# One 64-column product per level and chunk in the chunked HGRN2 recurrence, in place of merged 192-column products

## The chip, the cores and the metric

One core of a Trainium2 chip runs the whole kernel. The metric is the device time of one execution in microseconds (us). The kernel before took 1265.52 us, the median of three runs (1264.85 to 1266.1).

## What is computed

The reference is one decoder layer on 1024 tokens of width 1024, in float32: RMSNorm, one input projection (3584 columns), two head groups side by side, one output projection with residual, then RMSNorm, a SwiGLU feed-forward of hidden width 2816, residual and a last RMSNorm. Group A is dilated softmax attention with rotary positions (8 heads of 64). Group B, which the change touches, is HGRN2 (4 heads, state 128):

```python
f = lb + (1.0 - lb) * jax.nn.sigmoid(f_logit)
key = 1.0 - f
qf = jax.nn.silu(q)
# S_t = diag(f_t) S_{t-1} + (1 - f_t) i_t^T,  o_t = S_t^T q_t, computed chunkwise
scores = jnp.einsum('bhntd,bhnsd,bhntsd->bhnts', qc, kc, decay)   # decay = prod of f over (s, t]
o_intra = jnp.einsum('bhnts,bhnsv->bhntv', scores, vc)
```

followed by a per-head RMSNorm and a SiLU gate.

## The kernel before, in words

**Order of the work.** The kernel does not issue as it goes. `Prog` collects operations with their tiles; `schedule()` (from L141) is a list scheduler that gives each engine one fixed order, by classes (`P.cls`) and by the longest way to the end, with a cost for every operation. The recurrence (`hgrn`, class 0) goes before attention (class 1), and both go before the dense products (class 2) wherever they are ready. The cost of a product is written in `mm` (L274): a float32 product of n columns counts 4n/2400 + 0.008 us. All engines run their order strictly, so a change of any operation or cost may move others.

**Stages.** From about 30 to 390 us PE multiplies the input projection, written as Strassen products over pairs of 256 columns in the order `DENSE` (F0 K1 Q0 G0 Q1 R0 K0 I0 R1 F1 G1 V0), each operand split in a high and a low part ("wh", "wl"; DVE makes most low parts). From 187 us on, after I0, the four recurrence heads run one after the other (they share the buffers E14, E15, E16), and R1, F1, G1 and V0 are the dense work between them. Attention starts at 374 us, the output projection at about 550 us, and the feed-forward fills the rest.

**One recurrence head** (`hgrn`, from L824). The 1024 tokens are 8 chunks of 128. Inside a chunk, the matrix A of scores is built by doubling: level 0 joins neighbouring tokens, level l joins blocks of w = 2^l. `ks` (keys) is the stationary operand, `qp` (queries times decays) gives the columns. `grow(l, part)` multiplies half of `ks` ("k", L876), half of `qp` ("q", L873) and the block ends of `f` ("f", L881) by the decay of the neighbouring block. Every product of the recurrence is float32, 128 rows deep, with a 128x128 stationary operand.

Before the change the row `qc` (in E15) holds 8 chunks of 192 columns. For the diagonal and level 0 these are 128 query columns and the 64 of level 0. For the pairs of levels (1,2), (3,4) and (5,6) they are three blocks of 64: level l, level l+1, and the cross block, which the tensor_tensor of L900 makes. `scores` (L848) multiplies two chunks (2 x 192 columns) into one of the three PSUM banks "h" (5, 6, 7). DVE then multiplies the diagonal by the identity (L889), and `pred` (L856) copies 64 columns of two chunks at a time into A, under a mask of `lm` (L864). A level's `k` growth must wait for the products that read `ks`.

After the levels, `ks` is transposed, the chunk states are summed (L305), A and `qp` are multiplied with values and states, the gate `g_d` is fetched into A's place, and two DVE operations make the output (L305), which also free the buffers for the next head. `lm` is also the place of `yab`, the two staging halves of attention's output.

Of the kernel before, what the change touches and what calls it, by code (L numbers as in the profile page):

```python
# [12 lines left out]
I32 = mybir.dt.int32  # L13
AF = mybir.ActivationFunctionType
OP = mybir.AluOpType
# [4 lines left out]
S = 1024  # L20
# [3 lines left out]
NT = S // 128  # L24
# [222 lines left out]
def hymba_block(ctx: ExitStack, tc: tile.TileContext, x, norm1_w, w_in, lb_logits, hgrn_norm_w, w_out,  # L247
                norm2_w, w_gate_up, w_down, final_norm_w, cos, sin, amask, lmask, eye, out):
    nc = tc.nc
# [7 lines left out]
    P = Prog()  # L257
# [9 lines left out]
    def dma(o, i, nbytes, run=2048):  # L267
        r = [i] if isinstance(i, (View, Buf)) else []
        w = [o] if isinstance(o, (View, Buf)) else []
        gi = i if r else (lambda: i)  # L270
        go = o if w else (lambda: o)
        P.op("SP", 0.5, lambda: nc.sync.dma_start(go(), gi()), r, w, nbytes=moved(nbytes, run))

    def mm(items, r, w):  # L274
        cost = sum(4 * n / 2400.0 + 0.008 if f32 else n / 2400.0 + (0.0132 if n > 128 else 0.007)
                   for o, lt, rh, st, sp, n, m, f32 in items)

        def fn():
            for o, lt, rh, st, sp, n, m, f32 in items:
                nc.tensor.matmul(o(), lt(), rh(), start=st, stop=sp, skip_group_check=True)  # L280
        P.op("PE", cost, fn, r, w)
# [17 lines left out]
    def tt(eng, o, a, b, op, n, f=1.0):  # L299
        alts = two(n, bank_of(a) or bank_of(b) or bank_of(o) or op == OP.max)  # L300
        P.flex(alts, lambda e: ENG[e].tensor_tensor(o(), a(), b(), op=op), [a, b], [o])  # L301
# [60 lines left out]
    plus, minus = P.buf("plus", [128, 128], F32R), P.buf("minus", [128, 128], F32R)  # L362
    mhalf = P.buf("mhalf", [128, 8])
    P.op("DVE", 0.1, lambda: nc.vector.memset(mhalf(), -0.5), [], [mhalf])
    lm = P.buf("lm", [128, 10, 64], I32)

    def rstd_of(ss, n, width, tag):
        ms = P.buf("ms" + tag, [128, n])
# [21 lines left out]
    def bank(stream, shape=(128, 512)):  # L390
        names = BANKS[stream]
        while True:
            n = rot[stream] = rot.get(stream, -1) + 1
            tag = f"b{names[n % len(names)]}"
            if tag not in held:
                return P.buf(tag, list(shape), F32, "ps")
# [228 lines left out]
    hw = P.buf("hw", [128, 4])  # L625

    def consts():
        dma(lm, lmask, 128 * 640 * 4)
        for r in range(2):
            dma(tiny.v(lambda t, r=r: t[:, 4 * r:4 * r + 4]),  # L630
                bass.AP(tensor=lb_logits.tensor, offset=lb_logits.offset + r * 512, ap=[[1, 128], [128, 4]]), 2048)
        dma(hw, bass.AP(tensor=hgrn_norm_w.tensor, offset=hgrn_norm_w.offset, ap=[[1, 128], [128, 4]]), 2048)
        c = [tiny.v(lambda t, i=i: t[:, 4 * i:4 * i + 4]) for i in range(8)]
        tt("DVE", c[2], c[0], c[1], OP.max, 4)
        for r in range(2):
            tt("DVE", c[r], c[r], c[2], OP.subtract, 4)
        act(tiny.v(lambda t: t[:, 12:20]), tiny.v(lambda t: t[:, 0:8]), AF.Exp, 8)
        tt("DVE", c[2], c[3], c[4], OP.add, 4)
        P.op("DVE", 0.1, lambda: nc.vector.reciprocal(c[2](), c[2]()), [tiny], [tiny])
        tt("DVE", c[5], c[3], c[2], OP.mult, 4)  # L640
        ts("DVE", c[6], c[5], -1.0, 1.0, 4)
# [17 lines left out]
    for t in range(NT):  # L659
# [11 lines left out]
        u = us[t % 2]  # L671
# [152 lines left out]
    def hgrn(h):  # L824
# [5 lines left out]
        half = lambda v, g: v.buf.v(lambda t: v.get(t)[:, g * 512:g * 512 + 512], v.key + (g,))  # L830
        cs = lambda v, c: v.buf.v(lambda t: v.get(t)[:, c * 128:c * 128 + 128], v.key + (c // 4,))
        pj = lambda b, j: b.v(lambda t: t[:, j * 128:j * 128 + 128], j)
        qc = lambda a, n, g=None: E15.v(lambda t: t[:, S:].rearrange("p (c e) -> p c e", e=192)[
            :, slice(0, NT) if g is None else slice(4 * g, 4 * g + 4), a:a + n], (1, a) if g is None else (1, a, g))
        r128 = lambda v: sub(v, lambda a: a.rearrange("p (c e) -> p c e", e=128))

        def up(v, w, g=None):

            x = v if g is None else half(v, g)
            return sub(x, lambda a: a.rearrange("p (c b two e) -> p c b two e", e=w, two=2, b=64 // w)[:, :, :, 1, :])  # L840

        def blocked(v, w):
            return sub(v, lambda a: a.rearrange("p c (b e) -> p c b e", e=w))
        dma(f, f_d.v(lambda b: b[rs, :], h), 128 * S * 4)
        dma(qc(0, 128), q_d.v(lambda b: b[rs, :].rearrange("p (c e) -> p c e", e=128), h), 128 * S * 4, 512)
        dma(r128(iv), i_d.v(lambda b: b.rearrange("(c p) n -> p c n", p=128)[:, :, rs], h // 2), 128 * S * 4, 512)

        def scores(n, g):  # L848

            ps = bank("h", (128, 2, 192))  # L850
            mm([(ps.v(lambda b, c=c: b[:, c, :n]), cs(ks, 2 * g + c),
                 E15.v(lambda t, c=c: t[:, S + (2 * g + c) * 192:S + (2 * g + c) * 192 + n]),
                 True, True, n, 128, True) for c in range(2)], [half(ks, g // 2), E15.v(None, 1)], [ps])
            return ps

        def pred(g, ps, a, w, m):  # L856

            Ag = half(A, g // 2)
            nb = 64 // w

            def fn():
                Av = A().rearrange("p (c b two e) -> p c b two e", c=NT, two=2, e=w)[:, 2 * g:2 * g + 2, :, 1, :]
                mv = lm()[:, m, :].rearrange("p (b e) -> p b e", e=w)[:, None, :, :].to_broadcast([128, 2, nb, w])
                nc.vector.copy_predicated(Av, mv, ps()[:, :, a:a + 64].rearrange("p c (b e) -> p c b e", e=w))  # L864
            P.op("DVE", 0.2, fn, [ps, lm], [Ag])

        def grow(l, part):

# [12 lines left out]
                       lambda e: nc.vector.tensor_tensor(o(), o(), blk(f, 0)[:, :, w - 1:w], op=OP.mult), [f], [f])  # L881
        for g in range(2):
            ts("POOL", half(ks, g), half(f, g), -1.0, 1.0, 512)
            tt("DVE", r128(half(qp, g)), qc(0, 128, g), r128(half(f, g)), OP.mult, 512)
            act(qc(128, 64, g), sub(up(qp, 1, g), lambda a: a[:, :, :, 0]), AF.Copy, 256)
        for g in range(4):
            ps = scores(192, g)
            Ag = half(A, g // 2)
            P.op("DVE", 0.33, lambda g=g, ps=ps: nc.vector.tensor_tensor(  # L889
                A().rearrange("p (c e) -> p c e", e=128)[:, 2 * g:2 * g + 2, :], ps()[:, :, :128],  # L890
                ident()[:, None, :].to_broadcast([128, 2, 128]), op=OP.mult), [ps, ident], [Ag])
            pred(g, ps, 128, 1, 0)
        for part in "kqf":
            grow(0, part)
        for i, l in enumerate((1, 3, 5)):
            w = 1 << l
            act(blocked(qc(0, 64), w), up(qp, w), AF.Copy, 512)
            grow(l, "q")
            act(blocked(qc(64, 64), 2 * w), up(qp, 2 * w), AF.Copy, 512)
            P.flex([("DVE", 0.6, True)], lambda e, w=w: nc.vector.tensor_tensor(  # L900
                qc(128, 64)().rearrange("p c (b e) -> p c b e", e=2 * w), up(qp, 2 * w)(),
                f().rearrange("p (c b two e) -> p c b two e", c=NT, two=2, e=2 * w)[:, :, :, 0, 2 * w - 1:2 * w].to_broadcast(
                    [128, NT, 32 // w, 2 * w]), op=OP.mult), [qp, f], [qc(128, 64)])
            for g in range(4):
                ps = scores(192, g)
                pred(g, ps, 0, w, l)
                pred(g, ps, 64, 2 * w, l + 1)
                pred(g, ps, 128, 2 * w, 7 + i)
            for n in (l, l + 1):
                for part in "kqf":  # L910
                    if (n, part) != (l, "q"):
                        grow(n, part)
        dec = P.buf("dec", [128, NT])
        P.op("DVE", 0.08, lambda: nc.vector.tensor_copy(dec(), f().rearrange("p (c e) -> p c e", e=128)[:, :, 127]),
             [f], [dec])
# [415 lines left out]
def _consts():  # L1331
    half = 32
    inv = (10000.0 ** (-np.arange(half, dtype=np.float64) / half)).astype(np.float32)
    ang = (np.arange(S, dtype=np.float32)[:, None] * inv[None, :]).astype(np.float32)
    cos = np.ascontiguousarray(np.tile(np.cos(ang).astype(np.float32).T, (4, 1)))
    sin = np.ascontiguousarray(np.tile(np.sin(ang).astype(np.float32).T, (4, 1)))
    q = np.arange(128)[:, None]
    j = np.arange(1920)[None, :]
    d = q + 896 - j
    cnt = ((d >= 0) & (d <= 128)).astype(np.int64)  # L1340
    cnt += (d >= 0) & (d <= 512) & (d % 4 == 0)
    cnt += (d >= 0) & (d % 16 == 0)
    amask = np.where(cnt > 0, 8.0 * np.log(np.maximum(cnt, 1)), -1e30).astype(np.float32)
    s = np.arange(128)[:, None]
    t = np.arange(64)[None, :]
    lmask = np.stack([((s // w) % 2 == 0) & (s // (2 * w) == t // w) for w in (1, 2, 4, 8, 16, 32, 64)]
                     + [(s % (4 * w) < w) & (s // (4 * w) == t // (2 * w)) for w in (2, 8, 32)], axis=1)
    return {"cos": cos, "sin": sin, "amask": amask, "lmask": np.ascontiguousarray(lmask.astype(np.int32)),
            "eye": np.eye(128, dtype=np.float32)}

# [24 lines left out]
```

## Time and profile before

| what | value |
|---|---|
| median of three runs | 1265.52 us |
| the profiled execution, whole | 1265.95 us |
| its span, first to last instruction | 1264.2 us |
| PE busy | 1218.2 us, 6244 matmul records |
| DVE busy | 1031.6 us, 2121 instructions |
| ACT busy | 476.8 us |
| granted TensorE clock, mean | 0.993 |

A float32 product stands in the trace as two matmul records (two passes) and two weight loads; an fp32r product, as in the dense stage, is one of each. The busy time of PE is the union of records whose ends are modelled, and neighbouring records overlap: a matmul's duration is longer than its distance to the next. Distances are therefore read from the timeline, where a merged row gives the start of its first record, the time to the end of its last, and the count. "Granted clock" 1.00 is 2.4 GHz and 0.50 is 1.2 GHz.

### The profile page before, as it was taken

To read this page: it belongs to the slowest core of one execution; us is meant where nothing else is said; L and a number is where in the kernel's file an instruction comes from. 1 tells how busy PE (TensorE), PEld (TensorE's weight loads), DVE (VectorE), ACT (ScalarE), POOL (GpSimd) and SP (SyncE) were. 2 spreads that over 40 slices of the span, in tenths; PEclk is the share of its full clock that TensorE was granted. 3 is DMA by queue.
4 is the path that set the end of the run, shared out by engine and by line. 5 is a ranking of instruction groups with operands and counts; after the bars stand their busy time and mean duration, and the time that the engine had idled before them with its cause. 6 is when DMAs were issued, how large, how long until landed. Compare 5 with 4: busy or idle time off the path is not lost.

```text
span 1264.2 us, 17960 instructions
## 1 busy us (share of the span) xinstructions
PE 1218.2 (96%) x6244; PEld 1031.2 (82%) x6244; DVE 1031.6 (82%) x2121; ACT 476.8 (38%) x1019; POOL 114.1 (9%) x212
## 2 busy tenths in 40 slices
PE   5999999999998899999999999999999999999997
PEld 4878889888997788876788888888888887888885
DVE  6999989989789999946897766766766769978986
ACT  5642332345327888722642222222222223223232
POOL 1110000101004434400100000000000000000001
PEclk9999999999999999999999999999999999999998
DMA  8434443524557755114314313233223269534433
GB/s 263 137 121 168 167 152 106 167 76 151 161 182 254 205 141 143 36 42 148 134 52 149 113 67 121 97 104 117 100 84 125 84 226 394 179 100 132 132 107 121
DMA packets 132522, 175.57 MB, mean 139 GB/s; under 512 B 18512, under 2 KB 85200, under 8 KB 132432
## 3 DMA queue, kind: packets, MB, share of 16 engines
q1 hardware_dynamic: 132432, 174.43, 42.0%
q8 instruction: 49, 0.80, 0.3%
q14 instruction: 41, 0.34, 0.1%
HBM read 122.76 MB, written 51.64 MB: 138 GB/s over the span
## 4 chain that ended last, share of the span: by engine, by line
PE 79%; DVE 12%; DMA 4%; issue 2%; ACT 1%; POOL 1%; DVEq 0%; POOLq 0%; ACTq 0%; SPq 0%
PE b L280 77%; DVE E L301 3%; DVE wl L301 2%; PE b L1048 2%; DMA st<-in_w_in_dram 1%; DVE E L864 1%; DVE E L305 1%; DVE wh L1011 1%; DVE wh L301 1%; PE b L286 1%; DMA st<-in_w_out_dram 1%; DMA m_d<-lm 1%; DVE st L301 1%; DVE E L876 0%; DVE E L873 0%
## 5 line engine op out<-in xcount | busy, mean ns | idle before, releaser
L280 PE MATMUL b<-E,wh 128*128 128x512 f32 (+1 forms) x2096 | 644.9, 389 | 6.0 <-DVE E L301 4.1
L280 PEld LDWEIGHTS b<-E,wh 128*128 128x128 f32 x2096 | 385.6, 189 | 90.0 <-DVE E L301 7.0
L280 PE MATMUL b<-E,wl 128*128 128x512 f32 (+1 forms) x1048 | 404.5, 386 | 0.0
L347 ACT ACTIVATE wh<-st 128x512 fp32r<-128x512 f32 (+1 forms) x204 | 127.3, 627 | 393.3 <-PE b L280 221.4
L301 DVE TENSOR_TENSOR wl<-st,wh 128x512 fp32r<-128x512 f32 (+1 forms) x341 | 230.8, 687 | 4.6 <-ACT wh L347 1.4
L280 PEld LDWEIGHTS b<-E,wl 128*128 128x128 f32 x1048 | 197.5, 188 | 41.1 <-DVE wl L301 0.4
L301 DVE TENSOR_TENSOR E<-b,E 128x512 f32<-128x512 f32 (+1 forms) x165 | 110.9, 685 | 45.7 <-PE b L280 41.2
L349 DVE TENSOR_SCALAR wh<-st 128x512 fp32r<-128x512 f32 x122 | 51.5, 425 | 89.6 <-PE b L280 83.0
L280 PE MATMUL b<-wl,wh 128*128 128x512 f32 x308 | 119.9, 389 | 0.5 <-DVE wl L301 0.5
L280 PE MATMUL b<-wh,wl 128*128 128x512 f32 x308 | 119.9, 389 | 0.1
L280 PE MATMUL b<-wh,wh 128*128 128x512 f32 x308 | 119.8, 389 | 0.0
L280 PE MATMUL b<-wl,E 128*128 128x256 f32 (+1 forms) x544 | 116.3, 288 | 3.0 <-DVE wl L301 2.8
L280 PE MATMUL b<-E,E 128*128 128x192 f32 (+3 forms) x464 | 99.8, 325 | 3.5 <-DVE E L305 2.6
L301 DVE TENSOR_TENSOR wl<-b,wl 128x512 f32<-128x512 f32 (+2 forms) x139 | 89.3, 651 | 16.7 <-PE b L280 13.5
L301 DVE TENSOR_TENSOR st<-st 128x512 f32<-128x512 f32 x136 | 92.7, 687 | 0.7
L280 PEld LDWEIGHTS b<-wl,E 128*128 128x128 f32 x544 | 87.4, 191 | 6.3 <-DVE wl L301 3.7
L337 ACT ACTIVATE E<-E 128x512 f32<-128x512 f32 (+2 forms) x77 | 54.2, 704 | 95.2 <-DVE E L301 42.4
L280 PE MATMUL b<-wh,E 128*128 128x256 f32 x448 | 89.0, 290 | 0.2 <-DVE wh L301 0.2
L280 PEld LDWEIGHTS b<-E,E 128*128 128x128 f32 x464 | 75.7, 193 | 9.1 <-DVE E L305 2.8
L349 POOL TENSOR_SCALAR wh<-st 128x512 fp32r<-128x512 f32 (+1 forms) x17 | 11.3, 666 | 753.3 <-DVE E L301 505.4
L280 PEld LDWEIGHTS b<-wh,E 128*128 128x128 f32 x448 | 72.3, 192 | 0.8 <-DVE wh L301 0.4
L280 PEld LDWEIGHTS b<-wl,wh 128*128 128x128 f32 x308 | 57.8, 188 | 13.0 <-DVE wl L301 0.9
(140 smaller groups left out, 1394.6 us busy)
## 6 DMA issues: line engine op xcount, KB each, us to landing
st<-in_w_gate_up_dram SPq DMA_DIRECT2D x22, 1024.0 KB, 5.2
st<-a_d SPq DMA_DIRECT2D x77, 256.0 KB, 2.7
st<-in_w_in_dram SPq DMA_DIRECT2D x16, 1024.0 KB, 5.7
a_d<-E SPq DMA_DIRECT2D x45, 256.0 KB, 2.1
E<-in_w_down_dram SPq DMA_DIRECT2D x44, 256.0 KB, 5.3
E<-in_x_dram SPq DMA_DIRECT2D x8, 512.0 KB, 9.0
E<-qs_d SPq DMA_DIRECT2D x32, 128.0 KB, 3.6
E<-kh_d SPq DMA_DIRECT2D x32, 128.0 KB, 3.6
```

Of the source, the lines that this page charges most:

```text
L280: nc.tensor.matmul(o(), lt(), rh(), start=st, stop=sp, skip_group_check=True)
L286: nc.tensor.transpose(ov(), iv(), ident())
L301: P.flex(alts, lambda e: ENG[e].tensor_tensor(o(), a(), b(), op=op), [a, b], [o])
L305: lambda e: nc.vector.scalar_tensor_tensor(o(), a(), s(), b(), op0=op0, op1=op1), [a, s, b], [o])
L337: nc.scalar.activation(o(), a(), func, **kw)
L347: nc.scalar.activation(o(), i(), AF.Copy)
L349: ENG[e].tensor_scalar(o(), i(), 1.0, 0.0, op0=OP.mult, op1=OP.add)
L864: nc.vector.copy_predicated(Av, mv, ps()[:, :, a:a + 64].rearrange("p c (b e) -> p c b e", e=w))
L1011: nc.vector.tensor_tensor_reduce(pn(), pv(), am()[:, o:o + n], 1.0, -3e38 if mx is None else mx(), op0=OP.add, op1=OP.max, accum_out=m()),
L1048: nc.tensor.transpose(ov(), iv(), ident())
```

## The change

Each of the seven levels becomes one product of 64 columns for each chunk (8 per level), all into one bank, followed by one masked copy for all 8 chunks. The merged pairs, the cross block and its three masks go. The queries lie in one plain row `qr`, fetched in two halves; the columns of a level go into one of three small buffers `qu` in turn. The diagonal is one product of 128 columns for each chunk, four chunks to a bank.

```diff
-    lm = P.buf("lm", [128, 10, 64], I32)
+    lm = P.buf("lm", [128, 7, 64], I32)
...
-        dma(lm, lmask, 128 * 640 * 4)
+        dma(lm, lmask, 128 * 448 * 4)
...
+        qr = colv(E15, S, S, 1)
+        qu = [colv(E15, 2 * S, 512, 2), half(qr, 0), half(qr, 1)]
...
-        dma(qc(0, 128), q_d.v(lambda b: b[rs, :].rearrange("p (c e) -> p c e", e=128), h), 128 * S * 4, 512)
+        for g in range(2):
+            dma(half(qr, g), q_d.v(lambda b, g=g: b[rs, g * 512:g * 512 + 512], h), 128 * 512 * 4)
...
-        def scores(n, g):
-
-            ps = bank("h", (128, 2, 192))
-            mm([(ps.v(lambda b, c=c: b[:, c, :n]), cs(ks, 2 * g + c),
-                 E15.v(lambda t, c=c: t[:, S + (2 * g + c) * 192:S + (2 * g + c) * 192 + n]),
-                 True, True, n, 128, True) for c in range(2)], [half(ks, g // 2), E15.v(None, 1)], [ps])
-            return ps
-
-        def pred(g, ps, a, w, m):
...
+        def level(l):
+
+            w = 1 << l
+            u = qu[l % 3]
+            act(sub(u, lambda a: a.rearrange("p (c b e) -> p c b e", e=w, b=64 // w)), up(qp, w), AF.Copy, 512)
+            ps = bank("h")
+            mm([(ps.v(lambda t, c=c: t[:, c * 64:c * 64 + 64]), cs(ks, c), u.buf.v(lambda t, c=c: u.get(t)[:, c * 64:c * 64 + 64], u.key),
+                 True, True, 64, 128, True) for c in range(NT)], [ks, u], [ps])
...
+                Av = A().rearrange("p (c b two e) -> p c b two e", c=NT, two=2, e=w)[:, :, :, 1, :]
+                mv = lm()[:, l, :].rearrange("p (b e) -> p b e", e=w)[:, None, :, :].to_broadcast([128, NT, 64 // w, w])
+                nc.vector.copy_predicated(Av, mv, ps().rearrange("p (c b e) -> p c b e", c=NT, e=w))
+            P.op("DVE", 0.6, fn, [ps, lm], [A])
...
-            act(qc(128, 64, g), sub(up(qp, 1, g), lambda a: a[:, :, :, 0]), AF.Copy, 256)
-        for g in range(4):
-            ps = scores(192, g)
-            Ag = half(A, g // 2)
-            P.op("DVE", 0.33, lambda g=g, ps=ps: nc.vector.tensor_tensor(
-                A().rearrange("p (c e) -> p c e", e=128)[:, 2 * g:2 * g + 2, :], ps()[:, :, :128],
-                ident()[:, None, :].to_broadcast([128, 2, 128]), op=OP.mult), [ps, ident], [Ag])
-            pred(g, ps, 128, 1, 0)
-        for part in "kqf":
-            grow(0, part)
-        for i, l in enumerate((1, 3, 5)):
-            w = 1 << l
-            act(blocked(qc(0, 64), w), up(qp, w), AF.Copy, 512)
-            grow(l, "q")
-            act(blocked(qc(64, 64), 2 * w), up(qp, 2 * w), AF.Copy, 512)
-            P.flex([("DVE", 0.6, True)], lambda e, w=w: nc.vector.tensor_tensor(
-                qc(128, 64)().rearrange("p c (b e) -> p c b e", e=2 * w), up(qp, 2 * w)(),
...
-            for g in range(4):
-                ps = scores(192, g)
-                pred(g, ps, 0, w, l)
-                pred(g, ps, 64, 2 * w, l + 1)
-                pred(g, ps, 128, 2 * w, 7 + i)
-            for n in (l, l + 1):
-                for part in "kqf":
-                    if (n, part) != (l, "q"):
-                        grow(n, part)
+            tt("DVE", half(qp, g), half(qr, g), half(f, g), OP.mult, 512)
+            ps = bank("h")
+            mm([(pj(ps, j), cs(ks, 4 * g + j), cs(qr, 4 * g + j), True, True, 128, 128, True) for j in range(4)],
+               [half(ks, g), half(qr, g)], [ps])
+            P.op("DVE", 0.6, lambda g=g, ps=ps: nc.vector.tensor_tensor(
+                half(A, g)().rearrange("p (c e) -> p c e", e=128), ps().rearrange("p (c e) -> p c e", e=128),
+                ident()[:, None, :].to_broadcast([128, 4, 128]), op=OP.mult), [ps, ident], [half(A, g)])
+        for l in range(7):
+            level(l)
+            for part in "kqf":
+                grow(l, part)
```

## Rows read from the trace of the kernel before

**Rows 1.** The page: span, and busy time of each engine.
```profile
span 1264.2 us, 17960 instructions
PE 1218.2 (96%) x6244; PEld 1031.2 (82%) x6244; DVE 1031.6 (82%) x2121; ACT 476.8 (38%) x1019; POOL 114.1 (9%) x212
```

**Rows 2.** Windows: stretch, length, busy us (count) of PE, PEld, DVE, ACT, POOL; granted clock.
```profile
186.00:293.00 107.00, 106.75 (x663) 96.48 (x662) 96.75 (x237) 39.54 (x98) 8.95 (x10) 1.00 0.39 125
293.00:335.00 42.00, 41.18 (x266) 37.67 (x265) 40.58 (x103) 15.78 (x25) 1.53 (x1) 1.00 0.31 103
335.00:374.00 39.00, 35.80 (x262) 34.54 (x261) 27.74 (x67) 10.81 (x35) 3.05 (x3) 0.96 0.65 203
374.00:400.00 26.00, 24.00 (x178) 21.73 (x177) 25.84 (x91) 20.18 (x63) 8.50 (x18) 1.00 0.89 282
400.00:425.00 25.00, 18.65 (x112) 15.23 (x111) 22.46 (x56) 18.23 (x47) 12.28 (x24) 0.93 0.85 249
425.00:450.00 25.00, 24.34 (x159) 21.02 (x158) 24.36 (x87) 21.34 (x60) 9.96 (x21) 1.00 0.39 98
550.00:625.00 75.00, 69.05 (x321) 53.22 (x320) 49.85 (x82) 25.45 (x48) 6.39 (x13) 0.98 0.34 116
625.00:1250.00 625.00, 624.41 (x2762) 515.12 (x2761) 483.86 (x835) 165.71 (x293) 7.23 (x14) 1.00 0.38 130
```

**Rows 3.** Chain that ended last, 150 to 450 us: start, us, what.
```profile
343.98 4.91 DMA E<-g_d
...
354.56 0.34 DVE E L889
...
356.71 0.60 DVE E L900
...
360.18 1.56 DVE E L864 x7
...
399.61 7.93 DMA st<-in_w_out_dram
...
417.50 3.90 DMA m_d<-lm
```

**Rows 4.** Waits, 330 to 425 us: who waited for whom, total us, times, longest.
```profile
PE b L280 <- DVE mx L1011: 4.0, 4, 1.5
...
PE b L280 <- DVE E L305: 2.6, 1, 2.6
```

**Rows 5.** Timeline of PE, two recurrence bursts, a dense pair between: start, us, operation, count.
```profile
190.45 2.78 PE L280 MATMUL b<-E,E 128*128 128x192 f32 x16
...
195.34 0.28 PE L280 MATMUL b<-wl,E 128*128 128x256 f32 x1
195.46 0.40 PE L280 MATMUL b<-wh,E 128*128 128x256 f32 x2
...
226.78 1.72 PE L280 MATMUL b<-E,E 128*128 128x128 f32 x14
```

**Rows 6.** Timeline of PE and its weight loads, fp32r products in attention, 445.45 us on.
```profile
445.23 0.57 PE L280 MATMUL b<-wl,E 128*128 128x256 f32 x4
445.35 0.31 PEld L280 LDWEIGHTS b<-wl,E 128*128 128x128 f32 x2
...
445.58 0.19 PEld L280 LDWEIGHTS b<-E 128*128 128x128 f32 x1
...
445.63 0.33 PE L280 MATMUL b<-E 128*128 128x256 f32 x1
445.69 0.19 PEld L280 LDWEIGHTS b<-E,E 128*128 128x128 f32 x1
```

**Rows 7.** Groups by form, 180 to 420 us: count, busy us, mean ns, idle before.
```profile
L280 PE MATMUL b<-E,E 128*128 128x192 f32 x256 | 49.6, 337 | 3.5 <-DVE E L305 2.6 <-issue 0.5 <-DVE E L864 0.4
...
L337 ACT ACTIVATE E<-E 128x512 f32<-128x512 f32 x24 | 15.4, 641 | 44.6 <-DVE E L873 30.0 <-PE b L280 14.5
```

**Rows 8.** DMA issues: KB each, median us to landing.
```profile
E<-q_d SPq DMA_DIRECT2D x4, 512.0 KB, 4.5
```

More of the change, by code (lines that the diff above doesn't have):

```diff
@@ L832, in hgrn @@
         pj = lambda b, j: b.v(lambda t: t[:, j * 128:j * 128 + 128], j)
-        qc = lambda a, n, g=None: E15.v(lambda t: t[:, S:].rearrange("p (c e) -> p c e", e=192)[
-            :, slice(0, NT) if g is None else slice(4 * g, 4 * g + 4), a:a + n], (1, a) if g is None else (1, a, g))
+        qr = colv(E15, S, S, 1)
+        qu = [colv(E15, 2 * S, 512, 2), half(qr, 0), half(qr, 1)]
         r128 = lambda v: sub(v, lambda a: a.rearrange("p (c e) -> p c e", e=128))
@@ L840, in up @@
             return sub(x, lambda a: a.rearrange("p (c b two e) -> p c b two e", e=w, two=2, b=64 // w)[:, :, :, 1, :])
-        def blocked(v, w):
-            return sub(v, lambda a: a.rearrange("p c (b e) -> p c b e", e=w))
         dma(f, f_d.v(lambda b: b[rs, :], h), 128 * S * 4)
-        dma(qc(0, 128), q_d.v(lambda b: b[rs, :].rearrange("p (c e) -> p c e", e=128), h), 128 * S * 4, 512)
+        for g in range(2):
+            dma(half(qr, g), q_d.v(lambda b, g=g: b[rs, g * 512:g * 512 + 512], h), 128 * 512 * 4)
         dma(r128(iv), i_d.v(lambda b: b.rearrange("(c p) n -> p c n", p=128)[:, :, rs], h // 2), 128 * S * 4, 512)
-        def scores(n, g):
-            ps = bank("h", (128, 2, 192))
-            mm([(ps.v(lambda b, c=c: b[:, c, :n]), cs(ks, 2 * g + c),
-                 E15.v(lambda t, c=c: t[:, S + (2 * g + c) * 192:S + (2 * g + c) * 192 + n]),
-                 True, True, n, 128, True) for c in range(2)], [half(ks, g // 2), E15.v(None, 1)], [ps])
-            return ps
-        def pred(g, ps, a, w, m):
-            Ag = half(A, g // 2)
-            nb = 64 // w
+        def level(l):
[5 more added lines that the diff above has]
+                 True, True, 64, 128, True) for c in range(NT)], [ks, u], [ps])
             def fn():
[L862 to L865, printed above, removed]
+                Av = A().rearrange("p (c b two e) -> p c b two e", c=NT, two=2, e=w)[:, :, :, 1, :]
+                mv = lm()[:, l, :].rearrange("p (b e) -> p b e", e=w)[:, None, :, :].to_broadcast([128, NT, 64 // w, w])
+                nc.vector.copy_predicated(Av, mv, ps().rearrange("p (c b e) -> p c b e", c=NT, e=w))
+            P.op("DVE", 0.6, fn, [ps, lm], [A])
         def grow(l, part):
@@ L883, in hgrn @@
             ts("POOL", half(ks, g), half(f, g), -1.0, 1.0, 512)
-            tt("DVE", r128(half(qp, g)), qc(0, 128, g), r128(half(f, g)), OP.mult, 512)
-            act(qc(128, 64, g), sub(up(qp, 1, g), lambda a: a[:, :, :, 0]), AF.Copy, 256)
-        for g in range(4):
-            ps = scores(192, g)
-            Ag = half(A, g // 2)
-            P.op("DVE", 0.33, lambda g=g, ps=ps: nc.vector.tensor_tensor(
-                A().rearrange("p (c e) -> p c e", e=128)[:, 2 * g:2 * g + 2, :], ps()[:, :, :128],
-                ident()[:, None, :].to_broadcast([128, 2, 128]), op=OP.mult), [ps, ident], [Ag])
-            pred(g, ps, 128, 1, 0)
-        for part in "kqf":
-            grow(0, part)
-        for i, l in enumerate((1, 3, 5)):
-            w = 1 << l
-            act(blocked(qc(0, 64), w), up(qp, w), AF.Copy, 512)
-            grow(l, "q")
-            act(blocked(qc(64, 64), 2 * w), up(qp, 2 * w), AF.Copy, 512)
-            P.flex([("DVE", 0.6, True)], lambda e, w=w: nc.vector.tensor_tensor(
-                qc(128, 64)().rearrange("p c (b e) -> p c b e", e=2 * w), up(qp, 2 * w)(),
-                f().rearrange("p (c b two e) -> p c b two e", c=NT, two=2, e=2 * w)[:, :, :, 0, 2 * w - 1:2 * w].to_broadcast(
-                    [128, NT, 32 // w, 2 * w]), op=OP.mult), [qp, f], [qc(128, 64)])
-            for g in range(4):
-                ps = scores(192, g)
-                pred(g, ps, 0, w, l)
-                pred(g, ps, 64, 2 * w, l + 1)
-                pred(g, ps, 128, 2 * w, 7 + i)
-            for n in (l, l + 1):
-                for part in "kqf":
-                    if (n, part) != (l, "q"):
-                        grow(n, part)
+            tt("DVE", half(qp, g), half(qr, g), half(f, g), OP.mult, 512)
[9 more added lines that the diff above has]
+                grow(l, part)
         dec = P.buf("dec", [128, NT])
@@ L1345, in _consts @@
     t = np.arange(64)[None, :]
-    lmask = np.stack([((s // w) % 2 == 0) & (s // (2 * w) == t // w) for w in (1, 2, 4, 8, 16, 32, 64)]
-                     + [(s % (4 * w) < w) & (s // (4 * w) == t // (2 * w)) for w in (2, 8, 32)], axis=1)
+    lmask = np.stack([((s // w) % 2 == 0) & (s // (2 * w) == t // w) for w in (1, 2, 4, 8, 16, 32, 64)], axis=1)
     return {"cos": cos, "sin": sin, "amask": amask, "lmask": np.ascontiguousarray(lmask.astype(np.int32)),
```

## The prediction

> **What bounds the kernel now.** Read the page's first lines first: PE is busy 96% of the span, DVE 82% [rows 1]. That share is an average over stages, so the windows come next [rows 2]. From 625 us to the end PE is busy 624.41 of 625 us and no operation of the recurrence lies there. The stage that the change touches runs from 186 us (first recurrence head) to about 390 us. From 186 to 293 us PE is busy 106.75 of 107 us and DVE 96.75; from 293 to 335 us 41.18 and 40.58 of 42. So two engines are nearly full at once, with PE the fuller. From 335 us on gaps open: PE idles 3.2 us in 335 to 374, 2.0 in 374 to 400, 6.35 in 400 to 425 and 0.66 in 425 to 450. With the 0.25 and 0.8 us before them that is 13.3 us. The granted clock adds a little: a mean of 0.96 over 39 us and of 0.93 over 25 us, in two levels of 1.00 and 0.50, means 3.1 and 3.5 us at the low level, which lose half of that, 3.3 us. All that can be won back in this stage without taking work from PE is then 13.3 + 3.3 = 16.6 us.
>
> The chain of waits shows who causes these gaps: from 354 us it runs almost wholly over DVE's recurrence operations, and before that over the fetch of the gate [rows 3]. The list of waits names DVE for PE's idle time in the same stretch [rows 4]. So the stage has a PE that is nearly full, and a DVE chain that makes the gaps. The change takes work from DVE; whether it takes or gives work to PE is the question that decides.
>
> **PE, the first term.** Columns fall from 32 x 192 = 6144 a head to 8 x 128 + 56 x 64 = 4608, but products rise from 32 to 64. Before, 256 records of 192 columns [rows 7]: a burst of 16 takes 2.78 us to its last end [rows 5]; without the tail of one record (0.33) that is 15 distances of 0.163 us, so 256 x 0.163 = 41.8 us.
>
> After, the diagonal has 4 x 8 x 2 = 64 passes of 128 columns. The 14 passes of [rows 5] take 1.72 us; less 0.27 of tail, 13 distances of 0.111 us: 64 x 0.111 = 7.1 us.
>
> The levels have 4 x 7 x 8 x 2 = 448 passes of 64 columns, a shape that the trace does not have. By its columns a pass would take a third of 0.163, 0.054 us. But each pass needs its own weight load. [Rows 6] show what such a load costs when columns are few. The four products from 445.23 us are two of 256 and two of 128 columns; the next record starts at 445.63. The weight loads start at 445.35, 445.47 (the pair's end less 0.19), 445.58 and 445.69: 0.11 to 0.12 apart, although the columns of a 128-wide fp32r product need only about 0.06 us (256 columns take 0.12, the distance of the dense pair in [rows 5]). The load sets the pace, at 0.11 us. The 128-column float32 passes keep 0.111 as well, so nothing in the rows is faster. I take 0.111: 448 x 0.111 = 49.7 us. Sum for PE: 49.7 + 7.1 - 41.8 = **+15.0 us**. Ends: 0.054 gives 24.2 + 7.1 - 41.8 = -10.5 us; 0.12, the widest distance of [rows 6], gives +19.1 us.
>
> Against this stands a figure of the Trainium skill (TensorE: Matmul & The Clock Gate, Back-to-back issue gap): streams of weight load and 128-column matmul were measured there at about 81 ns each. By it an estimate of the sum would be 448 x 0.081 + 7.1 - 41.8 = +1.6 us. No row here shows such a pace with a load for every pass, so I stay with 0.111.
>
> **DVE, the second term.** Where DVE is the chain, an operation costs what the chain's pieces show [rows 3]: 7 masked copies in 1.56 us, 0.223 each; 0.60 for a 512-element tensor_tensor (L900); 0.34 for the 256-element diagonal (L889). Before: 160 copies (40 a head in the code) 35.7 us, 12 cross blocks 7.2, 16 diagonals 5.4, together 48.3. After: 28 copies of 512 elements, not in the trace; between 0.34 (256 elements) and 0.89 (four small ones), I take 0.60, the row of the same size: 16.8; 8 diagonals of 512 at 0.60: 4.8; together 21.6. DVE is relieved of **26.7 us** (18.6 to 34), some 6.7 a head. None of it is on PE's account where PE is full; it counts only in the gaps.
>
> **What of it comes back.** Of the 16.6 us in gaps, 2.6 are PE behind L305 [rows 4], which itself waits 4.91 us for the gate's fetch [rows 3]: the same fetch, by the same queue, stands there after the change. That leaves 14.0 us. Some is DVE pressure while the last head, V0 and the first attention heads overlap (DVE 25.84 of 26 us from 374 to 400 us [rows 2]); that should go. The largest piece, 400 to 425 us, is attention's start: its products wait for the score maxima (4.0 us [rows 4]), and the chain runs there through fetches of 7.93 and 3.90 us that the change leaves alone [rows 3]. A lighter DVE would get the first scores done earlier, not the fetches. I take half: **-7.0 us**; ends 0 and -14.0.
>
> **The small edits.** ACT: 8 copies of 256 and 24 of 512 elements become 28 of 512, at 0.64 us [rows 7] within a few us of before; ACT is busy 39.54 of 107 us [rows 2], which hides it; if uncovered, the four extra 512s would cost 2.6 us. The queries' fetch becomes two transfers where one took 4.5 us to land [rows 8]: four more issues on SP, ahead of the values' fetch and of the dense weights; they are issued a head ahead, and cost nothing unless SP is late. The mask fetch shrinks at the very start: nothing. Handovers between PE, ACT and DVE rise from 4 bursts a head to 9, but three column buffers in turn let ACT copy ahead, and a head has about 48 us, while seven levels of 16 passes (1.8 us), a growth of 0.6 and some 0.5 us of handover need 20. If the dense work between ran out, each extra handover would show. The scheduler prices a 64-column product at 4 x 64/2400 + 0.008 = 0.115 us, against the 0.222 that I expect. Its orders will have DVE wait at the one copy that needs all eight products, with dense low parts queued behind it, and PE's dense products wait for those. I put nothing on it in the sum, because DVE has 26.7 us more of slack, and keep it as a rival. Outside the stage only the output projection's start (550 to 625 us, 5.95 us of PE idle [rows 2]) could move: 0, within 2 us either way.
>
> **Sum.** +15.0 - 7.0 = +8.0 us. The profiled execution took 1265.95 us, 0.43 above the median of 1265.52; against the median the forecast is **1273.5 us**.
>
> **The rivals.**
> - *Weight loads don't pace the passes (faster).* If a load for 64 columns hides under the pass before, PE changes by -10.5 and the gaps by -7: 1248 us. Place: the level bursts. It decides below 0.095 us a pass, where 448 passes give 42.6 + 7.1 - 41.8 = +7.9, about what the gaps return. For it: no 64-column pass has been seen. Against: the four distances of [rows 6]. Chance 0.05. A middle pace of 0.083, halfway between 0.054 and 0.111, gives 37.2 + 7.1 - 41.8 = +2.5, less 7: 1261 us; chance 0.05. That is about the pace of the Trainium skill's page named above.
> - *The gaps close wholly (no change).* +15 - 14 = +1: 1266.5 us. For it: the chain is DVE's from 354 us on. Against: the fetches in the chain. Chance 0.12, a quarter of it below -2.5 us.
> - *Nothing comes back (slower still).* The scheduler's too-low price and nine handovers a head eat DVE's slack: +15 to +19 and up to 2 more: 1280.5 to 1287 us. For it: PE full to 293 us and DVE waiting in order. Chance 0.2.
> - The main case, +2.5 to +13: chance 0.58.
>
> **How the numbers follow.** 0.2%, about what a measurement can tell, is 2.5 us. Faster: 0.05 + 0.05 + 0.03 + 0.02 from the lower edge of the main case = 0.15. Same: 0.09 + 0.01 = 0.10. Slower: 0.75. The range leaves out about 0.1 on either side: from 1261 (the middle pace) to 1284 us (the middle of the last rival).
>
> **What would show it.** Right: 448 passes of 64 columns about 0.11 us apart and 16 in about 1.9 us, weight loads back to back; 28 masked copies near 0.6 us in a row; DVE some 25 us less busy between 186 and 400 us; V0's last product 8 to 15 us later; less PE idle from 374 to 425 us. Wrong: passes under 0.09 us; PE gaps from 186 to 335 us where there are none now; or a stage from 400 to 425 us as empty as before.

## The result and the profile after

The changed kernel takes **1273.51 us** (median of 4 runs, 1273.16 to 1273.9) against 1265.18 us (4 runs, 1262.98 to 1266.1) of the kernel before in the same session: a ratio of **1.0069, 95% interval 1.0051 to 1.0086**. It is slower by some 8 us. The profiled execution took 1273.16 us, with a span of 1271.4 us, 7.2 us above the span of [rows 1].

The page of the kernel after, first its span and the busy time of each engine, then the chain that ended last:

```profile
span 1271.4 us, 18328 instructions
...
PE 1225.4 (96%) x6500; PEld 1043.9 (82%) x6500; DVE 1017.9 (80%) x1987; ACT 475.2 (37%) x1011; POOL 109.2 (9%) x198
...
PE 89%; DVE 5%; DMA 3%; ACT 1%; issue 1%; SPq 0%; POOL 0%; DVEq 0%; POOLq 0%; ACTq 0%
```

The same line of the page of the kernel before:

```profile
PE 79%; DVE 12%; DMA 4%; issue 2%; ACT 1%; POOL 1%; DVEq 0%; POOLq 0%; ACTq 0%; SPq 0%
```

The chain has moved: DVE's share fell from 12 to 5%, PE's rose from 79 to 89%. The kernel is slower because PE has more to do, not because another engine holds it up. Where DVE lost its share is seen in the chain of the stretch 150 to 366 us, its share by line, first before (the view cuts the line off), then after; the chain after is PE's alone from 189 us on:

```profile
by line: PE b L280 61.4%; DVE E L301 6.4%; DVE wl L301 5.2%; DVE E L864 3.5%; DMA E<-f_d 2.7%; issue 2.5%; DMA E<-g_d 2.3%; DVE st L301 2.1%; DVE wh L301 1.8%; DVE E L876 1.7%; PE b L286 1.7%; DVE E L873 1.5%; DVE E L305 1.5%; DMA f_d<-wh 1
```
```profile
by line: PE b L280 85.1%; DVE E L301 4.5%; PE b L286 2.4%; DMA kl_d<-E 2.3%; DVE wl L301 1.8%; DMA E<-q_d 1.8%; DVE st L301 1.1%; DVE wh L301 0.6%; issue 0.3%; SPq L272 0.2%; DVE wh L349 0.0%; DVEq L301 0.0%
```

The waits from 186 to 374 us (who waited for whom, us in total, times, longest) say the same of the `k` growth, L876 before and L871 after:

```profile
DVE E L876 <- PE b L280: 1.6, 2, 1.5
```
```profile
DVE E L871 <- PE b L280: 16.5, 21, 1.2
```

Before, the chain from 354 us on ran over DVE [rows 3]. After, DVE's growth operation waits 21 times for the level's products: the two engines have changed roles.

The new operations. The first fence is the timeline around the first level of the first head (start, us, operation, count); the second holds groups by form, 180 to 420 us (busy us, mean ns, idle before); the third DVE's timeline, the masked copies of levels 0, 1 and 2 of that head:

```profile
190.52 1.86 PEld L280 LDWEIGHTS b<-E,E 128*128 128x128 f32 x16
190.52 2.00 PE L280 MATMUL b<-E,E 128*128 128x64 f32 x16
...
193.48 1.89 PE L280 MATMUL b<-E,E 128*128 128x64 f32 x16
```
```profile
L280 PE MATMUL b<-E,E 128*128 128x64 f32 x448 | 53.1, 272 | 0.0
...
L859 DVE COPY_PREDICATED E<-lm,b 128x512 f32<-128x512 int32 x28 | 24.9, 891 | 0.0
```
```profile
193.17 1.30 DVE L859 COPY_PREDICATED E<-lm,b 128x512 f32<-128x512 int32 x1
196.75 1.32 DVE L859 COPY_PREDICATED E<-lm,b 128x512 f32<-128x512 int32 x1
200.32 0.70 DVE L859 COPY_PREDICATED E<-lm,b 128x512 f32<-128x512 int32 x1
```

Sixteen passes take 1.89 to 2.00 us, and their weight loads lie back to back. From one start to the next the median of the 64-column passes is 0.112 us. The copies of levels 0 and 1, whose targets are runs of one and two elements, take 1.3 us, those of the other levels 0.70 to 0.75.

The windows (columns as in [rows 2]):

```profile
186.00:293.00 107.00, 106.77 (x756) 99.04 (x755) 82.43 (x152) 38.09 (x93) 7.37 (x8) 1.00 0.37 121
293.00:335.00 42.00, 42.00 (x294) 38.90 (x293) 35.99 (x66) 15.11 (x24) 0.00 (x0) 1.00 0.37 120
335.00:374.00 39.00, 39.00 (x342) 39.00 (x341) 30.75 (x57) 13.01 (x38) 3.10 (x3) 1.00 0.55 168
374.00:400.00 26.00, 22.05 (x178) 21.14 (x176) 15.05 (x42) 12.12 (x39) 5.97 (x8) 1.00 0.91 317
400.00:425.00 25.00, 16.71 (x90) 13.43 (x91) 23.33 (x68) 15.94 (x45) 6.46 (x13) 0.80 0.63 175
425.00:450.00 25.00, 24.02 (x159) 20.92 (x158) 23.01 (x77) 20.45 (x57) 9.87 (x19) 1.00 0.68 179
...
625.00:1250.00 625.00, 624.41 (x2774) 515.83 (x2774) 485.95 (x836) 171.31 (x303) 7.40 (x14) 1.00 0.38 129
```

From 186 to 374 us PE is now busy but for 0.23 us, at a granted clock of 1.00; in 335 to 374 us it ran 342 records where it ran 262 before. From 374 to 425 us it is idle 12.2 us, where it was 8.35, and the mean granted clock from 400 to 425 us is 0.80 where it was 0.93 [rows 2].

**An account of PE.** Recorded ends are modelled and stretch over short waits, so I also took each product's distance to the next start, less the usual distance of its shape (0.226 us at 512 columns, 0.170 at 384, 0.162 at 192, 0.118 at 256, 0.111 below that). What is over is PE time lost. This is my own reckoning, from the records of one profiled execution each, and good to perhaps 1 us a cell; the last columns are from experiments told below. Only distances longer than usual are added up, not the shorter ones beside them, so scatter of unhindered products is in it too: after the change 4.8 us stand for 186 to 374 us, where the windows leave PE 0.23 us idle. Taken with their sign, long against short, the distances of that stretch lose 11.6 us before and 2.3 after. The stretches are fixed in time, and what lies in them moves as a kernel gets longer.

| PE time lost, us | before | after | copies twice | before, fewer copies | after, fewer copies | after, x later |
|---|---|---|---|---|---|---|
| 0 to 186 | 10.1 | 8.5 | 9.0 | 10.9 | 9.5 | 10.9 |
| 186 to 374 | **14.9** | **4.8** | **14.6** | 12.5 | **4.4** | 4.2 |
| 374 to 425 | **15.4** | **18.3** | 16.1 | 16.2 | 19.5 | 13.5 |
| 425 to 450 | 3.3 | 3.4 | 6.5 | 3.6 | 3.5 | 11.4 |
| 450 to 625 | 18.9 | 18.4 | 16.6 | 17.5 | 19.0 | 17.7 |
| from 625 | 2.9 | 3.2 | 7.3 | 3.0 | 3.3 | 5.8 |
| sum | 65.6 | 56.5 | 70.0 | 63.6 | 59.1 | 63.6 |
| PE work (sum of the usual distances) | 1183.3 | 1198.7 | 1198.7 | 1183.3 | 1198.7 | 1198.7 |
| span | 1264.2 | 1271.4 | 1285.4 | 1262.4 | 1274.0 | 1279.4 |

PE's work grew by 15.4 us and its losses fell by 9.1, which gives 6.3 of the 7.2 us. The losses fell in the recurrence, by 10.1 us between 186 and 374 us; attention's start became 2.9 us worse. Landmarks of the trace say the same: V0's last product came 10.0 us later (383.9 to 393.9 us), the last masked copy 14.8 earlier (383.7 to 368.9), the first product with the values 16.5 later (390.6 to 407.1), the first fetch of the gate and up weights 8.7 later (576.7 to 585.4). Of the 16.5 us by which the values are used later, 10.0 are V0's own delay, and 6.5 lie behind V0.

Where the 6.5 us come from is seen on SP's queue: DMA issues of the transfers of the residual x, of w_out and of the values v, first before, then after (start, us of issuing, transfer, count):

```profile
375.76 0.45 SPq L272 DMA_DIRECT2D E<-in_x_dram  x1
...
383.15 0.36 SPq L272 DMA_DIRECT2D wl<-v_d  x1
...
392.91 0.39 SPq L272 DMA_DIRECT2D E<-in_x_dram  x1
```
```profile
380.00 0.91 SPq L272 DMA_DIRECT2D E<-in_x_dram  x2
...
392.05 0.44 SPq L272 DMA_DIRECT2D st<-in_w_out_dram  x1
392.59 1.30 SPq L272 DMA_DIRECT2D E<-in_x_dram  x2
395.46 4.64 SPq L272 DMA_DIRECT2D wl<-v_d  x2
```

The recurrence's buffers E14 to E16 come free earlier, and the x transfers that wait for free buffers go out: four of 1 MB stand ahead of the first fetch of the values where one stood before. Two of the four had landed by 391 us, before that fetch was issued (DMA issues from 379.9 to 381 us after: count, KB each, median us to landing):

```profile
E<-in_x_dram SPq DMA_DIRECT2D x2, 1024.0 KB, 9.0
```

The other two, and 1 MB of w_out, were still under way; before, the x transfer had landed, and w_out alone was under way. The fetch is then a link of the chain (365 to 430 us of the kernel after; start, us, what), and takes 9.62 us where the first one took 3.9 before:

```profile
395.46 9.62 DMA wl<-v_d
```

### The profile page after: what moved, and what is told of

Read it like the earlier page. It is cut to its first block, busy times and chain, and to the rows that moved or that the text cites. A ratio compares the mean times of both kernels' runs of the same rounds, so it can differ in the third digit from the quotient of the medians.

```text
span 1271.4 us, 18328 instructions
## 1 busy us (share of the span) xinstructions
PE 1225.4 (96%) x6500; PEld 1043.9 (82%) x6500; DVE 1017.9 (80%) x1987; ACT 475.2 (37%) x1011; POOL 109.2 (9%) x198
## 4 chain that ended last, share of the span: by engine, by line
PE 89%; DVE 5%; DMA 3%; ACT 1%; issue 1%; SPq 0%; POOL 0%; DVEq 0%; POOLq 0%; ACTq 0%
PE b L280 85%; DVE E L301 3%; PE b L1025 2%; DMA st<-in_w_in_dram 2%; PE b L286 1%; DMA wl<-v_d 1%; DVE wl L301 1%; DVE E L305 1%; DMA kl_d<-E 0%; SPq L272 0%; DMA E<-q_d 0%; DVE wh L988 0%; ACT E L347 0%; DVE wh L301 0%; DVE st L301 0%
## 5 line engine op out<-in xcount | busy, mean ns | idle before, releaser
L280 PE MATMUL b<-E,E 128*128 128x64 f32 (+3 forms) x720 | 111.4, 283 | 0.2 <-DMA E<-q_d 0.2
L301 DVE TENSOR_TENSOR wl<-b,wl 128x512 f32<-128x512 f32 (+2 forms) x139 | 89.7, 653 | 20.2 <-PE b L280 16.6
L280 PEld LDWEIGHTS b<-E,E 128*128 128x128 f32 x720 | 94.4, 192 | 2.5 <-issue 0.4
L337 ACT ACTIVATE E<-E 128x512 f32<-128x512 f32 (+1 forms) x73 | 53.3, 730 | 93.1 <-DVE E L301 44.5
L349 POOL TENSOR_SCALAR wh<-st 128x512 fp32r<-128x512 f32 (+1 forms) x17 | 10.8, 634 | 720.3 <-DVE E L301 505.4
```

The lines of the kernel that those rows point to most:

```text
L337: nc.scalar.activation(o(), a(), func, **kw)
L349: ENG[e].tensor_scalar(o(), i(), 1.0, 0.0, op0=OP.mult, op1=OP.add)
```

## The experiments

Each kernel ran beside the kernel before on its own chip, whose median lay between 1264.1 and 1266.6 us, so ratios are compared. The kernel after stands at 1.0069, 1.0051 to 1.0086.

**1. Do the columns or the weight loads pace a pass?** The kernel after with 32 of each level's 64 columns; the copy is made twice on those 32, so that DVE keeps its load (29.2 us of recorded copies in place of 24.9).

```
-  t[:, c * 64:c * 64 + 64] ... u.get(t)[:, c * 64:c * 64 + 64]
+  t[:, c * 64:c * 64 + 32] ... u.get(t)[:, c * 64:c * 64 + 32]
```

> The kernel after, with 32 of the 64 columns in each level product and each masked copy made twice on those 32 columns (so DVE does about the same); half of the level scores are left out. All orders are kept. Theory W (a weight load paces each pass at 0.11 us): the 448 passes stay 0.11 us apart and the time stays within 2 us of 1273.5. Rival C (columns pace the passes): 448 x 0.027 us less, about 12 us faster, 1261.5 us.

1274.36 us, ratio 1.0071 (1.0049 to 1.0093). The timeline of PE, one burst:

```profile
193.72 1.86 PE L280 MATMUL b<-E,E 128*128 128x32 f32 x16
```

Half the columns, the same 1.86 us: from 32 to 128 columns a float32 pass with a load of its own costs 0.11 us. The columns don't pace it; that the weight load does is seen in run 4.

**2. What does DVE's load cost?** The kernel after with each masked copy issued twice, the order kept.

```
   nc.vector.copy_predicated(Av, mv, ps()...)
+  nc.vector.copy_predicated(Av, mv, ps()...)
```

> The kernel after, with each of the 28 masked copies issued twice; orders kept, result unchanged. DVE gets back 28 x 0.73 to 0.89 = 20 to 25 us between 193 and 370 us, about what the change had taken from it. Theory W (the lighter DVE closed the gaps before 374 us): 4 to 8 us slower than after, 1278 to 1281 us, with PE gaps from 186 to 374 us back. Rival O (the gaps closed because the order is another, DVE has slack): at most 1 us slower, 1274.5 us.

1286.64 us, ratio 1.0178 (1.0154 to 1.0202): some 13 us above the kernel after, for 24.7 us of recorded copies. Windows:

```profile
186.00:335.00 149.00, 144.64 (x982) 131.24 (x981) 127.01 (x220) 49.74 (x112) 7.39 (x8) 0.99 0.35 114
335.00:374.00 39.00, 37.11 (x314) 36.28 (x314) 34.96 (x62) 13.76 (x40) 2.05 (x2) 1.00 0.60 188
```

PE's gaps are back (4.36 and 1.89 us idle), and in the account its losses between 186 and 374 us return to 14.6 us. Cut at V0's last product in place of fixed times, 11.0 us more than after the change are lost between 186 us and that product and 2.4 behind it; most of the 7.3 us from 625 us on are lost ahead of the feed-forward, which starts 14 us later than after the change. The direction was as expected, the size about double.

**3. Was it the scheduler's low price?** The kernel after with a float32 product charged with what it takes.

```
-  cost = sum(4 * n / 2400.0 + 0.008 if f32 else ...
+  cost = sum(max(4 * n / 2400.0 + 0.008, 0.222) if f32 else ...
```

> The kernel after, with the scheduler charging 0.222 us for a 64-column float32 product in place of 0.115; nothing else. Theory W: the price only orders the work, the weight loads stay: within 2 us of 1273.5. Rival S (the low price makes the order bad, above all at attention's start at 400 us): 3 to 6 us faster, 1267.5 to 1270.5 us.

1274.29 us, ratio 1.0074 (1.0051 to 1.0096): no difference. The rival falls.

**4. PE's term alone.** The kernel before, with each 192-column product issued as 128 and 64 columns: PE gets the passes of the change, DVE keeps its old load.

```
-  nc.tensor.matmul(o(), lt(), rh(), ...)
+  for a, b in ((0, 128), (128, 192)): nc.tensor.matmul(o()[:, a:b], lt(), rh()[:, a:b], ...)
```

> The kernel before, with each 192-column product issued as 128 and 64 columns on the same keys; orders, copies and result unchanged. 256 passes of 0.163 become 512 of 0.111: Theory W: PE gets 512 x 0.111 - 41.8 = 15.0 us more, with DVE as it was, so 9 to 15 us slower than before, 1274 to 1280 us. Rival C (columns pace): no change, 1265.2 us.

1273.07 us (1271.79 to 1279.05), ratio 1.0074 (1.0045 to 1.0103). The timeline of PE, one burst:

```profile
189.79 3.68 PE L281 MATMUL b<-E,E 128*128 128x128 f32 x32
```

Less a tail of 0.27 these are 31 distances of 0.110 us on the mean; in turn they are 0.112, 0.165, 0.112 and 0.058, the last between the two passes of a 64-column product. The weight loads of the same burst do not follow this turn:

```profile
189.68 3.66 PEld L281 LDWEIGHTS b<-E,E 128*128 128x128 f32 x32
```

Less a tail of 0.19 they start 0.112 us apart. So a 64-column pass can start 0.058 us ahead of the next, and it is the load for each pass that holds the mean at 0.11.

PE's work in the account is 1198.7 us, as after the change. The profiled run was the slowest of its four, with a span of 1277.2 us. By the account it lost 13.5 us from 186 to 374 us, but some 6 of these are the distances of 0.165, which those of 0.058 make up for. Taken with their sign, the distances there lose 7.5 us, against 11.6 before and 2.3 after the change: in this execution PE's longer work alone covers some 4 us of the waits, with DVE's load as it was, and the change covers 5 more. The median is 6 us below that run and cannot be told from the kernel after: by the medians PE's passes alone cost 9 us (6 to 13 by the interval), as much as the whole change. So this run does not by itself show that DVE's relief gave anything.

**5. DVE's term alone.** The kernel before without its 48 copies of cross blocks.

```
   def fn():
+      if m > 6:
+          return
```

> The kernel before, with the 48 masked copies of the cross blocks left out (so a part of the scores is missing); products, orders and all other work as before. DVE loses 48 x 0.223 = 10.7 us between 198 and 384 us, PE nothing. Theory W (DVE's load makes part of PE's gaps before 390 us): 2 to 6 us faster than before, 1259 to 1263 us. Rival O (gaps come from the order, not from DVE's load): no change.

1261.91 us, ratio 0.9962 (0.9948 to 0.9975) against 17 runs of the kernel before: 4.8 us gained for 48 x 0.223 = 10.7 us of DVE's chain. The profiled execution, the slowest of its six, shows 2.4 us of them between 186 and 374 us. This shows what run 4 could not: before the change, PE waits for DVE's load, and less of it is time won.

**6. The same relief after the change.** The kernel after without 16 of its 28 copies.

```
+  if l in (1, 3, 5, 6):
+      return
   nc.vector.copy_predicated(Av, mv, ps()...)
```

> The kernel after, with 16 of its 28 masked copies left out (levels 1, 3, 5 and 6 of every head; their scores are missing from the output). By the 0.73 us that the copies of these levels take in the profile after, 11.7 us of VectorE work go, as many as the kernel before lost with its 48 cross-block copies (48 x 0.223 = 10.7), which made it 4.8 us faster. Theory W (after the change PE is the bound from 186 to 374 us and VectorE's work has no more gaps to give back there): no more than 0 to 2.5 us faster than the kernel after, a ratio of 1.005 to 1.007, PE busy in all but 2 us of 186 to 374 us as now. Rival G (the stage still stands on VectorE's load, and each us taken from it brings what it brought before): 4 to 6 us faster than the kernel after, a ratio of 1.002 to 1.004.

1275.4 us, ratio 1.0079 (1.0062 to 1.0096): nothing gained, although with level 1 at 1.31 us each more went than was reckoned, 14 us. Windows:

```profile
186.00:335.00 149.00, 149.00 (x1051) 138.21 (x1050) 111.52 (x207) 53.33 (x118) 7.37 (x8) 1.00 0.36 120
335.00:374.00 39.00, 39.00 (x342) 39.00 (x341) 28.04 (x52) 13.06 (x38) 3.10 (x3) 1.00 0.57 172
```

By the records PE is never idle from 186 to 374 us. Runs 2, 5 and 6 together: DVE's load costs time before the change, nothing more is to be had by lowering it after, and raising it again costs at once. After the change none of that gain is left to be had, and PE's 15.4 us of work stand against it. How much of it the relief bought, and how much PE's longer work would have covered without it, run 4 leaves open.

**7. Less of PE's term.** The kernel after, with the diagonal and level 0 in one 192-column product per chunk as before, the other six levels by themselves: 64 passes fewer. A column slice takes its group late, so all those products read the columns of chunks 2 and 3; the scores of the diagonal and of level 0 are therefore other numbers, the work is the same.

```
-  mm([(pj(ps, j), cs(ks, 4 * g + j), cs(qr, 4 * g + j), ..., 128, 128, True) for j in range(4)], ...)
+  mm([(ps.v(lambda b, c=c: b[:, c, :]), cs(ks, 2 * g + c), E15.v(... 192 columns ...), ..., 192, 128, True) for c in range(2)], ...)
...
-  for l in range(7):
+  for l in range(1, 7):
```

> The kernel after, with the diagonal and level 0 again one product of 192 columns for each chunk, as before the change; levels 1 to 6 as after; result unchanged. PE: 128 passes of 0.111 become 64 of 0.163, 3.8 us less; DVE about equal. Theory W: 2 to 5 us faster than after, 1269 to 1271.5 us. Rival C: columns are the same, no change, 1273.5 us.

1273.06 us, ratio 1.0045 (1.0032 to 1.0058): by the ratios 3 us under the kernel after, where the account has 3.8 us less PE work. The intervals overlap a little; the size fits.

**8 to 10. Is the fetch of the values worth its time?** The four x transfers behind the first two heads of attention, in the kernel after (8) and in the kernel before (9); then in the kernel after three of them behind the first fetch of the values (10).

```
   attention(h, js)
+  if (h, js) == (1, (0, 1, 2)):
+      for i in range(4): P.op("SP", 0.5, ... x[... 2 * i:2 * i + 2 ...], [ys[0]], [b], ...)
...
-  for i in range(4): dma(b, x[... 2 * i:2 * i + 2 ...], 1 << 20)
```

> The kernel after, with the four 1 MB transfers of the residual rows put behind the first two attention heads in the order (they lie ahead of the fetch of attention's values after the change, one of four before it); result unchanged. Theory X (the recurrence frees its buffers earlier, that lets these transfers start ahead of the values' fetch, which takes 9.6 us and holds attention's start): 3 to 6 us faster than after, 1267.5 to 1270.5 us, with the fetch near 4 us. Rival L (attention's start is slow by its own chain): within 1.5 us of after.

1279.2 us, ratio 1.0096 (1.0081 to 1.0111): by the ratios some 3 us slower than the kernel after, with intervals that overlap a little. The chain, and SP's queue:

```profile
397.84 4.31 DMA wl<-v_d
```
```profile
428.00 2.62 SPq L1062 DMA_DIRECT2D E<-in_x_dram  x4
```

The fetch fell from 9.62 to 4.31 us and the loss from 374 to 425 us from 18.3 to 13.5, as its theory has it. But the 4 MB then went out in one lump at 428 us, and the loss from 425 to 450 us rose from 3.4 to 11.4: the output projection's early products, which fill PE there, began at 446.6 us instead of 426.4.

> The kernel before, with the same four transfers put behind the first two attention heads; result unchanged. Theory X: only one of the four lies ahead of the values' fetch, so 0 to 2 us faster than before. Rival L: no change. Faster than before would make it the better of all so far.

1269.29 us, ratio 1.0019 (1.0009 to 1.0030): slower too, where a gain or nothing was expected.

> The kernel after, with three of the four 1 MB transfers of the residual rows put behind the first values' fetch (the first one stays ahead, since the output projection's filler needs it from 426 us); result unchanged. Theory X (the transfers that the earlier end of the recurrence lets start hold the values' fetch): 3 to 5 us faster than after, a ratio of 1.003 to 1.0045, with the fetch near 5 us and no new gap from 425 to 450 us. Rival L: within 1.5 us of after, ratio 1.0069.

1274.31 us, ratio 1.0075 (1.0056 to 1.0093): no gain. The first fetch still took 6.89 us, behind one x transfer and one of w_out, and the three after it took 7 to 10 us. The loss from 374 to 425 us fell by 2.3 us, and 3.4 us more were lost from 425 to 625 us. So the late fetch is real, but the transfers that delay it are needed soon after: in the two places tried, putting them elsewhere moves the wait.

**11 and 12. The change in the last head alone.** The kernel before with its fourth head written as after the change, and the true price of run 3, since the chain of [rows 3] ran over DVE in that head; then the same with three x transfers behind the values' fetch.

```
+  if h in (3,):
+      ...  (the body of the kernel after)
+  else:
+      ...  (the body of the kernel before)
```

> The kernel before, with the fourth recurrence head alone done as after the change (the scheduler charging 0.222 us for its products); result unchanged. Theory W: PE gets a quarter of 15 us, 3.75 us more, and the gaps from 335 to 374 us, 6 us larger before than after, close: 0 to 3 us faster than before, ratio 0.998 to 1.000. Rival (the gaps close only when all heads are lighter): 3 to 4 us slower, ratio 1.003.

1276.36 us (1271.34 to 1277.74; the profiled one 1271.43), ratio 1.0088 (1.0064 to 1.0112).

> As the run with the fourth head alone, and three of the four residual transfers behind the first values' fetch; result unchanged. Theories W and X together: 2 to 6 us faster than before, ratio 0.995 to 0.998, the best so far. If X falls: as without it.

1276.22 us, ratio 1.0093 (1.0071 to 1.0116). Both expectations of a gain were wrong. PE's work grew by only 3.9 us, but the losses did not fall: in the profile of run 11 they are 14.9 us from 186 to 374 us, and a transfer of the values on the way to attention takes as long as their fetch after the change (chain):

```profile
394.91 9.53 DMA v_d<-wh
```

The order is planned anew over the whole stage, and this order is a worse one; which of its moves costs the time was not separated, and stays open. So these runs don't tell which of the heads the gain in the recurrence comes from. No version with the whole of the work beat the kernel before.

## Why the prediction was right, and where not

The time was forecast at 1273.5 us and came at 1273.51, and the likeliest case was the one that happened. That agreement is better than the reasons were: the first term came out, and the second had the right size from the wrong place, which is luck.

**PE's term, +15.0: right.** 448 passes at 0.112 us, where 0.111 was taken from the distances of the loads in [rows 6]; the account has +15.4. Run 1 shows that columns are not the reason, since 32 cost the same, and run 4 that the loads are. Run 7 takes 64 passes away again, and is faster by about their size. The Trainium skill's rule (TensorE: Matmul & The Clock Gate, Back-to-back issue gap), some 81 ns for a load and a matmul of 128 columns, is not what these float32 passes do: the measurement decides. Another section of that page of the Trainium skill (LDWEIGHTS) fits them: a load takes its columns divided by 1.2, in ns. For 128 columns an estimate by it is 107 ns, near the 0.111 to 0.112 us measured.

**DVE's term, −26.7: mis-sized.** Copies of 512 elements were priced at 0.60 us, after a tensor_tensor of that size; they took 0.73, and 1.3 for levels 0 and 1. The 28 and the 8 diagonals are 24.9 + 5.5 = 30.4 us of recorded time, not 21.6. Against the 48.3 us of the old operations that is a relief of 17.9 us, just under the low end of 18.6 that the prediction gave. DVE's total fell by only 13.7 us (1031.6 to 1017.9). The edit takes 132 copies, 12 cross blocks and 8 diagonals from it, 152 instructions; the page counts 134 fewer. POOL runs 14 fewer and ACT 8 fewer, of which the edit explains 4: so 18 operations that may run on either engine went to DVE, most of them attention's operations on one element a partition. That part of the relief was spent by the scheduler, and the prediction left it out; what it cost was not tried. The sign named for this term came out even so: from 186 to 400 us DVE is busy 164.2 us where it was 190.9, 26.7 less. But some of that is attention's work, which moved behind 400 us.

**"What of it comes back", −7.0: the size held, the place was wrong.** This is the step that failed. The prediction read the gaps from PE's idle time and the clock [rows 2]. By these, 186 to 374 us had 4.27 + 1.56 = 5.83 us to give, of which 2.6 behind L305 were held to stay with the gate's fetch; 10.8 of the 14.0 us lay behind 374 us. The account has 10.1 us back between 186 and 374 us (9.3 with signs): some 4 of them before 335 us, where the records leave 1.07 us idle, and 6 from there to 374. The wait that was held to stay went too. Before, DVE waited for the gate, and PE behind it (186 to 374 us):

```profile
DVE E L305 <- DMA E<-g_d: 5.7, 1, 5.7
```

After the change neither that wait nor one of PE for L305 is in the list of the same stretch. And attention's start, which was to gain, lost 2.9 us instead. So the half of 14.0 us was a good number for a wrong reason. Nor is it shown that DVE's relief gave all of it: run 4 has some 4 us of these waits covered by PE's longer work, and by its medians nearly all of what comes back.

**The small edits.** The two query transfers cost nothing that shows; PE's only idle time behind one is 0.2 us. What the step on SP's queue did not ask is what a faster DVE would trigger: it frees the recurrence's buffers 15 us earlier, and with them 4 MB of x ahead of the values, half of it still under way when they are fetched. Runs 8 and 10 show that the delay is real, and that it was not won back by moving x to either of two places.

**The rivals.** Weight loads that don't pace the passes: refuted by runs 1 and 4. Gaps that close wholly: in the recurrence they nearly did, in attention not. Nothing comes back, through the scheduler's price and the extra handovers: refuted by the time itself; run 3 takes the price out of it. Of the signs named, the pace, the 16 passes in 1.9 us, the loads back to back, DVE's busy time and V0's last product (10 us later, 8 to 15 forecast) came out; the copies near 0.6 us and the fuller PE from 374 to 425 us did not. One of the signs of being wrong was there: from 400 to 425 us PE idles 8.29 us, not less than the 6.35 before.

## What to carry to other kernels

A float32 pass with a weight load of its own had a least time here that fewer columns didn't lower, so cutting 192 columns into 128 + 64 adds a load and saves nothing: count loads before columns when PE is the fuller engine. When PE's busy share is near one, don't read its slack from idle time; add up start-to-start distances against the shape's usual distance, long and short ones alike, and that shows what a neighbour's relief can still give back. Relief of an engine paid here until the other engine was the chain; beyond that, what showed of it were the moves of the scheduler and the queues.

## What the runs showed of the hardware that was not expected

- A float32 pass with its own weight load started 0.112 us after the one before it at 64 columns and at 32, 0.111 at 128 and 0.163 at 192.
- A masked copy of 512 elements a partition took 0.70 to 0.75 us when its target runs were 4 elements or longer and 1.3 us when they were 1 or 2; four of 128 elements in the old kernel took 4 x 0.223 = 0.89 together [rows 3].
- A 256 KB fetch took 9.62 us with three transfers of 1 MB under way at its issue (two of x, one of w_out; after), 6.89 with two (run 10), and 4.31 (run 8) and 3.9 (before) with w_out's alone.
- After the change DVE is busy 118.42 of 149 us from 186 to 335 us, and yet 24.7 us of copies more cost 13 us of the whole: an engine with a fifth of its time free was no cover for them. Some 14 us of copies less gained nothing.
